# Second MLP products: a written TensorE order, weights made inside the step before, and their sums on VectorE

## The chip, the cores and the metric

The kernel runs on one core of a Trainium2 chip. A core has TensorE (PE in the profile) for matrix products, VectorE (DVE), ScalarE (ACT) and GpSimd (POOL) for elementwise work, and SyncE (SP), whose queue issues most transfers. The metric is device time in microseconds (us), the median of several runs.

## What is computed

Two sequences of 512 tokens and width 1024 pass a trunk of two layers in fp32. Layer 0 mixes tokens by a Fourier transform, layer 1 by attention; each is followed by the same kind of MLP:

```python
def sq_relu_mlp(h, w_up, w_down):
    a = jnp.maximum(h @ w_up, 0)
    return (a * a) @ w_down

# in trunk(), for each layer i
        x = x + fourier_mix(rms_norm(x, fourier_norm[j]), fourier_w_out[j])    # layer 0
        x = x + gqa_attention(rms_norm(x, attn_norm[j]), ...)                  # layer 1
        x = x + sq_relu_mlp(rms_norm(x, mlp_norm[i]), mlp_w_up[i], mlp_w_down[i])
```

`w_up` is 1024 x 4096 and `w_down` 4096 x 1024. The change is in the product with `w_down`, the second product of each MLP.

## The kernel before

**Arithmetic.** Every fp32 operand is split into a high and a low half (`split`, L81 to L83): ScalarE casts the high half (L82), VectorE subtracts it from the operand (L83). One fp32 product is three matmuls (high x high, high x low, low x high). `halves` (L98) splits a raw weight tile into a buffer of its own and gives back two operands.

**Seven products for eight.** Both MLP products are done by blocks of 2 x 2 with seven products in place of eight, and so need sums of blocks. The first product (`first_product`, L811) works by pairs of `D_FF` columns; of a pair's four results `Pair.out` (L914) makes the differences t1 to t4 on GpSimd (L918 to L921) and `put` (L815) writes seven activation operands, b11, b21, b22, t1 to t4, to DRAM: b ones from ScalarE's queue, t ones from SP's (L818).

**The second product** (`second_product`, L1036) runs over groups of pairs (four wide; layer 1 has one two wide) and, within a group, over four blocks of output columns, m = 0 to 3. A step (m, group) is of one of two kinds:

- `row` (L1084): the raw weights are split, and two products, with b11 and b21, add up in one bank of PSUM. The bank is read after the first into e (`add_e`), and after the second into the residual (`add`, L1055).
- `sums` (L1094): weights are summed, two sums by VectorE (L1098, L1099) and two by GpSimd (L1100, L1101), split, and five products follow in three banks: t2, t1, t3, b22, t4; t1 and b22 share a bank, and so do t3 and t4, each read twice by VectorE.

`add` and `add_e` are called evacuations below. A product is 12 matmuls of 128x512 (6 in a two-wide group). A row step goes with the sums step beside it; the sums of the last two column blocks of layer 0 have none, and of the first group all four rows come first, two at a time (`two_rows`, L1180). When a group begins, `group` (L1125) fetches its activation operands from DRAM (L1045, SP's queue) and splits them, all at once: two tiles of 128x1024 for each operand. With the last step of a column block, L1208 and L1209 add e, and `ready` begins the next layer's norm on that block (L87, squares on GpSimd at L155); `late` loads and splits weights of attention.

**What sets the order.** Each engine runs its instructions in order. The order is a scheduler's, which plans from estimated times, save within `manual_schedule(engines=...)`, where the named engines follow the code. In `second_product` only `two_rows` is written out so. Raw weights have five buffers, split ones four, PSUM eight banks, activations and residuals share 38.

Of the kernel before, what the change touches and what calls it, by code (L numbers as in the profile page):

```python
# [40 lines left out]
def trunk_kernel(ctx, tc, x_in, xt_in, y_out, dcos, dsin, feat, rope, gfour, gcol, grow, gfin,  # L41
# [56 lines left out]
    def halves(raw, n=512):  # L98
        hi, lo = own()
        split(hi[:, : 2 * n], lo[:, : 2 * n], raw)  # L100
        return [(hi[:, i * n : (i + 1) * n], lo[:, i * n : (i + 1) * n]) for i in range(2)]
# [709 lines left out]
    def first_product(l, blocks, rows, ahead):  # L811
# [3 lines left out]
        def put(op, p, src):  # L815
            for g, (p0, n) in enumerate(ROW_GROUPS[l] if op in ROW else SUM_GROUPS[l]):
                if p0 <= p < p0 + n:
                    (nc.scalar if op in ("b11", "b21", "b22") else nc.sync).dma_start(spill[l][op][g][p - p0], src)  # L818
# [7 lines left out]
        class Pair:  # L826
# [87 lines left out]
            def out(self, b11, b12, b21, b22):  # L914
# [3 lines left out]
                nc.gpsimd.tensor_sub(t[:, 0], b12, b11)  # L918
                nc.gpsimd.tensor_sub(t[:, 1], b22, t[:, 0])
                nc.gpsimd.tensor_sub(b12, b22, b12)  # L920
                nc.gpsimd.tensor_sub(t4, b21, t[:, 1])  # L921
                for op, x in (("b11", b11), ("b21", b21), ("b22", b22), ("t1", t[:, 0]), ("t2", t[:, 1]),
                              ("t3", b12), ("t4", t4)):
                    put(op, p, x)
# [85 lines left out]
        for p, pair in enumerate(pairs[:-1]):  # L1010
# [12 lines left out]
            pair.out(*done)  # L1023
# [12 lines left out]
    def second_product(l, blocks, rows, late=lambda: None, ready=lambda m: None):  # L1036
# [47 lines left out]
        def row(m, g, n, b):  # L1084
            x0 = residual(0, m)
            a11, a12 = rows_early.pop(m, None) or halves(row_raw(m, g, n), n * P)
            o = ps()
            product(o, a11, b["b11"])
            add_e(m, o)
            product(o, a12, b["b21"], False)  # L1090
            add(x0[:, 0], o)

        def sums(m, g, n, b):
            x0, x1 = residual(0, m), residual(1, m)  # L1094
            x, y = sums_raw(m, g, n)
            a12, a21, a11, a22 = x[:, 0], x[:, 1], y[:, 0], y[:, 1]
            s = rawp.tile([P, 2, n * P], F32, tag="raw", name=nm("raw"))
            nc.vector.tensor_add(s[:, 1], a21, a22)  # L1098
            nc.vector.tensor_sub(s[:, 0], s[:, 1], a11)  # L1099
            nc.gpsimd.tensor_sub(a11, a11, a21)  # L1100
            nc.gpsimd.tensor_sub(a12, a12, s[:, 0])  # L1101
            s2, s1 = halves(s, n * P)
            s3, a22 = halves(y, n * P)
            hi, lo = own()
            s4 = hi[:, : n * P], lo[:, : n * P]
            split(*s4, a12)
            o6, o5, o7 = ps(), ps(), ps()
            product(o6, s2, b["t2"])
            add_e(m, o6)
# [596 lines left out]
```

## Time and profile before

| | us |
|---|---|
| median of 3 runs | 1772.12 (1770.47 to 1773.23) |
| profiled execution, its own time | 1768.37 |
| its span | 1766.2 |
| TensorE busy | 1695.8 |
| VectorE busy | 1239.8 |
| ScalarE busy | 871.5 |
| GpSimd busy | 485.5 |

The profile is of one execution. In its second part (40 equal slices, each digit the busy share in tenths) TensorE reads 9 nearly throughout. The matmuls at L808 are those of both MLPs; layer 0's second products fill 431 to 760 us, layer 1's 1429 to 1707. A row of the timeline joins work of one line that runs without a break; the bracket at its end says how long the engine stood idle before it and which instruction released it.

### The profile page before, as it was taken

Reading aid. Unit: us, or ns where it says so; the run is one execution under the profiler, and the core shown is the slowest. Engines: PE = TensorE matmul, PEld = TensorE weight load, DVE = VectorE, ACT = ScalarE, POOL = GpSimd, SP = SyncE. Lnnn points to the kernel's source line nnn. Section 1 sums busy time; section 2 is a strip of 40 time slices with the busy share of each in tenths; the row PEclk is TensorE's granted clock in tenths of the full one; section 3 lists DMA queues with packets and bytes.
Section 4 is the critical chain, followed back from the end, with each engine's and each line's share of the span. In section 5 each row is a group of like instructions: output and inputs, shape, how many; then the busy total and the mean of one; then the engine's idle time right before and its main releaser. Section 6 shows DMA issues by size and latency. Waiting matters only on the chain. (4 is left out here: it accounts for less than half of the span.)

```text
span 1766.2 us, 22070 instructions
## 1 busy us (share of the span) xinstructions
PE 1695.8 (96%) x7870; PEld 1395.5 (79%) x7870; DVE 1239.8 (70%) x1775; ACT 871.5 (49%) x1530; POOL 485.5 (27%) x384
## 2 busy tenths in 40 slices
PE   4999999999899999999999999999999999999997
PEld 4887788888787877778877888787888877878776
DVE  8768876545967768976578843697655478686765
ACT  6666444446333424546687724554544554243234
POOL 3330443231412111543334302114322242111104
PEclk9999999999999999999999999999999999999999
DMA  9823454448744534430100212224544596355232
GB/s 278 226 95 120 178 192 177 163 167 293 259 167 157 202 130 179 153 117 25 48 25 1 92 53 113 95 103 185 200 149 153 200 321 225 136 208 177 85 108 96
DMA packets 104150, 267.13 MB, mean 151 GB/s; under 512 B 10200, under 2 KB 10200, under 8 KB 104040
## 3 DMA queue, kind: packets, MB, share of 16 engines
q1 hardware_dynamic: 88200, 234.78, 37.1%
q10 hardware_dynamic: 14112, 25.70, 3.8%
q0 software_dynamic: 1728, 5.24, 1.7%
q8 instruction: 62, 1.02, 0.2%
q14 instruction: 48, 0.39, 0.1%
HBM read 190.70 MB, written 73.92 MB: 150 GB/s over the span
## 5 line engine op out<-in xcount | busy, mean ns | idle before, releaser
L808 PE MATMUL ps<-u,w 128*128 128x512 f32 x4872 | 1130.6, 392 | 25.7 <-DVE u L1055 11.7
L808 PEld LDWEIGHTS ps<-u,w 128*128 128x128 f32 x4872 | 912.8, 189 | 236.4 <-issue 12.0
L82 ACT CAST w<-raw 128x1024 fp32r<-128x1024 f32 (+2 forms) x242 | 228.5, 954 | 498.3 <-PE ps L808 324.8
L83 DVE TENSOR_TENSOR w<-raw,w 128x1024 fp32r<-128x1024 f32 (+2 forms) x238 | 272.4, 1148 | 65.8 <-ACT w L82 64.8
L83 DVE TENSOR_TENSOR u<-u,u 128x1024 fp32r<-128x1024 f32 x133 | 180.4, 1374 | 18.4 <-ACT u L82 17.8
L1055 DVE TENSOR_TENSOR u<-ps,u 128x512 f32<-128x512 f32 x160 | 109.8, 687 | 92.6 <-PE ps L808 92.2
L82 ACT CAST u<-u 128x1024 fp32r<-128x1024 f32 x133 | 135.0, 1042 | 66.8 <-DMA u<-spill_b 53.1
L77 PE MATMUL ps<-u,u 128*128 128x512 f32 (+2 forms) x424 | 162.8, 386 | 2.1 <-DVE u L600 1.2
L1100 POOL TENSOR_TENSOR raw<-raw,raw 128x512 f32<-128x512 f32 (+1 forms) x32 | 46.9, 1466 | 425.5 <-DVE raw L1099 394.0
L78 PE MATMUL ps<-u,u 128*128 128x512 f32 (+2 forms) x424 | 158.1, 373 | 5.7 <-DVE u L83 5.4
L918 POOL TENSOR_TENSOR u<-u 128x512 f32<-128x512 f32 x30 | 40.2, 1340 | 436.4 <-ACT u L824 436.4
L79 PE MATMUL ps<-u,u 128*128 128x512 f32 (+2 forms) x424 | 157.9, 372 | 1.9 <-POOL u L83 1.4
L155 POOL TENSOR_TENSOR t<-t,t 128x512 f32<-128x512 f32 (+1 forms) x56 | 79.6, 1425 | 184.7 <-ACT t L153 128.7
L78 PEld LDWEIGHTS ps<-u,u 128*128 128x128 f32 x424 | 82.9, 195 | 18.6 <-DVE u L83 8.6
L79 PEld LDWEIGHTS ps<-u,u 128*128 128x128 f32 x424 | 82.5, 195 | 15.8 <-POOL u L83 2.0
L77 PEld LDWEIGHTS ps<-u,u 128*128 128x128 f32 x424 | 82.6, 195 | 14.3 <-DVE u L600 1.8
L83 DVE TENSOR_TENSOR u<-ps,u 128x512 fp32r<-128x512 f32 (+4 forms) x126 | 76.5, 627 | 17.3 <-ACT u L82 16.1
L808 PE MATMUL ps<-u,u 128*128 128x512 f32 x360 | 86.8, 390 | 1.8 <-DVE t L896 1.8
L881 DVE TENSOR_TENSOR t<-ps,u 128x512 f32<-128x512 f32 x30 | 20.8, 692 | 91.4 <-PE ps L808 89.9
L808 PEld LDWEIGHTS ps<-u,u 128*128 128x128 f32 x360 | 67.4, 188 | 16.8 <-issue 2.9
L82 ACT CAST u<-ps 128x512 fp32r<-128x512 f32 (+4 forms) x126 | 66.4, 542 | 25.6 <-PE ps L79 14.6
L791 DVE TENSOR_TENSOR u<-ps,u 128x512 f32<-128x512 f32 (+1 forms) x48 | 30.9, 645 | 65.3 <-PE ps L79 65.3
(221 smaller groups left out, 2079.9 us busy)
## 6 DMA issues: line engine op xcount, KB each, us to landing
raw<-w_up SPq DMA_DIRECT2D x82, 512.0 KB, 3.8
u<-spill_t SPq DMA_DIRECT2D x60, 512.0 KB, 6.2
raw<-w_sum SPq DMA_DIRECT2D x56, 512.0 KB, 3.7
spill_t<-u SPq DMA_DIRECT2D x90, 256.0 KB, 2.0
u<-spill_b SPq DMA_DIRECT2D x45, 512.0 KB, 5.8
spill_b<-t ACTq DMA_DIRECT2D x60, 256.0 KB, 2.0
raw<-w_row SPq DMA_DIRECT2D x28, 512.0 KB, 3.3
park<-u SPq DMA_DIRECT2D x24, 512.0 KB, 3.3
```

The source lines that it names most:

```text
L77: nc.tensor.matmul(out, lh, rh, start=first, stop=False)
L78: nc.tensor.matmul(out, lh, rl, start=False, stop=False)
L79: nc.tensor.matmul(out, ll, rh, start=False, stop=last)
L82: nc.scalar.copy(dst_hi, src)
L83: eng.tensor_sub(dst_lo, src, f32(dst_hi))
L155: nc.gpsimd.tensor_add(acc[q][:, :n], acc[q][:, :n], s[:, :n])
L791: nc.vector.tensor_add(x[:, :n], o[:, :n], x[:, :n])
L808: nc.tensor.matmul(o, w[x][:, sl], h[k][y], start=first and k + i == 0, stop=k == n - 1 and i == 2, skip_group_check=not first)
L881: nc.vector.tensor_add(u2, ob, t[:, 0])
L918: nc.gpsimd.tensor_sub(t[:, 0], b12, b11)
L1055: nc.vector.tensor_add(x, o, x)
L1100: nc.gpsimd.tensor_sub(a11, a11, a21)
```

## The change

`second_product` is written anew around two classes, `Row` and `Sums`, and a loop with TensorE's order written out:

- A step's products stand as: the row's first, t1, t3, the row's second, t2, b22, t4. Between the two products of a bank stand two others, or three where the step has a row.
- The next step's weights are made inside a step: its loads are issued after t1, its row is split after the row's second, three of its four sums are made and the first split after t2, the fourth after b22; the split of the third pair stands at the beginning of its own step.
- All four sums are VectorE's. Split weights of two-wide steps live in an activation slot (`narrow`).
- Activation operands change one at a time: `change` fetches the next group's operand behind the last product that uses it, and `hook`, called between products, splits it three calls later.
- At layer 0's beginning TensorE's, ScalarE's and VectorE's orders are written: the firsts of four rows, then their four seconds, with the first sums step's weights between.
- The last pair's differences go to VectorE, in both layers; the spills of t1 to t4 of layer 0's last pair but one go on GpSimd's queue; eight low halves of w_qkv (128x1024) go from GpSimd to VectorE.

The core of the diff:

```diff
-            def out(self, b11, b12, b21, b22):
+            def out(self, b11, b12, b21, b22, eng=nc.gpsimd, queue=nc.sync):
...
-                nc.gpsimd.tensor_sub(t[:, 0], b12, b11)
...
+                eng.tensor_sub(t[:, 0], b12, b11)
...
-            pair.out(*done)
+            pair.out(*done, queue=nc.sync if last or p < np_ - 2 else nc.gpsimd)
...
-            pairs[-1].out(*done)
+            pairs[-1].out(*done, nc.vector)
...
-            nc.gpsimd.tensor_sub(a11, a11, a21)
-            nc.gpsimd.tensor_sub(a12, a12, s[:, 0])
...
+            def sum_123(self):
+                a21, a11, a22 = self.x[:, 1], self.y[:, 0], self.y[:, 1]
+                s = self.s = rawp.tile([P, 2, self.n * P], F32, tag="raw", name=nm("raw"))
+                nc.vector.tensor_add(s[:, 1], a21, a22)
+                nc.vector.tensor_sub(s[:, 0], s[:, 1], a11)
+                nc.vector.tensor_sub(a11, a11, a21)
...
+            def sum_4(self):
+                nc.vector.tensor_sub(self.x[:, 0], self.x[:, 0], self.s[:, 0])
...
+        def change(op, i, g):
+
+            if g + 1 < len((ROW_GROUPS, SUM_GROUPS)[i][l]):
+                later.append([0, op, g + 1, fetch(op, g + 1, (ROW_GROUPS, SUM_GROUPS)[i][l][g + 1][1])])
...
+            with tc.manual_schedule(engines={ET.PE, ET.Activation, ET.DVE}):
+                for r in rows:
+                    r.load()
+                    r.split()
+                sums.load()
+                rows[0].first()
+                rows[1].first()
+                put(*there_later[0])
+                sums.sum_123()
+                sums.sum_4()
+                rows[2].first()
+                rows[3].first()
+                for r, step in zip(rows, (sums.split_12, sums.split_4, sums.split_3, lambda: None)):
+                    r.second()
+                    step()
...
+        def hook():
+            for x in later:
+                x[0] += 1
+            if later and later[0][0] > 2:
+                _, op, g, h = later.pop(0)
+                b.pop(op, None)
+                put(op, h)
+                held[op] = g
+
+        for k, (rows, sums) in enumerate(items):
+            nrows, nsums = items[k + 1] if k + 1 < len(items) else ([], None)
...
+            with tc.manual_schedule(engines={ET.PE}):
+                for r in rows:
+                    r.first()
...
+                for r in nrows:
+                    r.load()
+                if k:
+                    sums.split_3()
+                hook()
+                for i, op in enumerate(("t1", "t3", "t2", "b22", "t4")):
+                    sums.go(i)
+                    if sums.m == 3:
+                        change(op, 1, sums.g)
+                    if i == 0 and nsums:
+                        nsums.load()
+                    if i == 1:
+                        for r in rows:
+                            r.second()
...
+                        hook()
+                        for r in nrows:
+                            r.split()
+                    hook()
...
+                    if i == 2 and nsums:
+                        nsums.sum_123()
+                        nsums.split_12()
+                    if i == 3 and nsums:
+                        nsums.sum_4()
+                        nsums.split_4()
...
-        ws = wkv if cg == 2 else [load_w(w_qkv[cg, u], nc.gpsimd, home=own if u < 2 else lent) for u in range(4)]
+        ws = wkv if cg == 2 else [load_w(w_qkv[cg, u], home=own if u < 2 else lent) for u in range(4)]
```

How the order of instructions stands at three places (line, operation, out<-in by the program's names with their numbers, shape). `ps` is a bank, `w` a split weight, `raw` a raw or summed one, `u` an activation slot.

*The beginning of layer 0's second products.* Before, on VectorE, from the low halves of the last two rows' weights on:

```order
L83 TENSOR_TENSOR w_627_3947<-raw_597_3808,w_627_3947 128x1024
L83 TENSOR_TENSOR w_628_3963<-raw_599_3812,w_628_3963 128x1024
L1098 TENSOR_TENSOR raw_629_4014<-raw_606_3824,raw_607_3826 128x512
L1099 TENSOR_TENSOR raw_629_4014<-raw_629_4014,raw_607_3826 128x512
L83 TENSOR_TENSOR u_583_3694<-u_583_3694,u_582_3693 128x1024
L83 TENSOR_TENSOR u_585_3697<-u_585_3697,u_584_3696 128x1024
L83 TENSOR_TENSOR u_602_3817<-u_602_3817,u_601_3816 128x1024
L83 TENSOR_TENSOR u_604_3820<-u_604_3820,u_603_3819 128x1024
L1055 TENSOR_TENSOR u_581_3691<-ps_623_3878,u_581_3691 128x512
L83 TENSOR_TENSOR u_609_3829<-u_609_3829,u_608_3828 128x1024
L83 TENSOR_TENSOR u_611_3832<-u_611_3832,u_610_3831 128x1024
L1055 TENSOR_TENSOR u_598_3810<-ps_624_3879,u_598_3810 128x512
```

and on GpSimd, the sums of the first summed step and the last pair's differences:

```order
L1100 TENSOR_TENSOR raw_607_3826<-raw_607_3826,raw_606_3824 128x512
L1101 TENSOR_TENSOR raw_606_3824<-raw_606_3824,raw_629_4014 128x512
L918 TENSOR_TENSOR u_617_3860<-u_566_3606 128x512
L919 TENSOR_TENSOR u_617_3860<-t_593_3736,u_617_3860 128x512
L920 TENSOR_TENSOR u_566_3606<-t_593_3736,u_566_3606 128x512
L921 TENSOR_TENSOR t_618_3861<-t_596_3804,u_617_3860 128x512
```

After, on VectorE, behind the same two low halves:

```order
L922 TENSOR_TENSOR u_617_3860<-u_566_3606 128x512
L923 TENSOR_TENSOR u_617_3860<-t_593_3736,u_617_3860 128x512
L924 TENSOR_TENSOR u_566_3606<-t_593_3736,u_566_3606 128x512
L925 TENSOR_TENSOR t_618_3861<-t_596_3804,u_617_3860 128x512
L83 TENSOR_TENSOR u_583_3694<-u_583_3694,u_582_3693 128x1024
L83 TENSOR_TENSOR u_585_3697<-u_585_3697,u_584_3696 128x1024
L1126 TENSOR_TENSOR raw_627_3918<-raw_606_3824,raw_607_3826 128x512
L83 TENSOR_TENSOR u_602_3817<-u_602_3817,u_601_3816 128x1024
L1127 TENSOR_TENSOR raw_627_3918<-raw_627_3918,raw_607_3826 128x512
L83 TENSOR_TENSOR u_604_3820<-u_604_3820,u_603_3819 128x1024
L1128 TENSOR_TENSOR raw_607_3826<-raw_607_3826,raw_606_3824 128x512
L1134 TENSOR_TENSOR raw_606_3824<-raw_606_3824,raw_627_3918 128x512
```

The four differences and all four sums now stand on VectorE, ahead of or among the splits of the activation operands; GpSimd has no work in this stretch.

*A step with a row in layer 0's second group.* On TensorE, the first row of each product or part of one (ten or so rows follow it with the same bank). Before:

```order
L808 MATMUL ps_669_4329<-u_646_4184,w_668_4326 128x512
L808 MATMUL ps_677_4376<-u_576_3681,w_674_4367 128x512
L808 MATMUL ps_669_4329<-u_650_4194,w_668_4326 128x512
L808 MATMUL ps_677_4376<-u_577_3682,w_674_4367 128x512
L808 MATMUL ps_678_4377<-u_582_3693,w_674_4367 128x512
L808 MATMUL ps_679_4378<-u_601_3816,w_675_4370 128x512
L808 MATMUL ps_678_4377<-u_608_3828,w_676_4373 128x512
L808 MATMUL ps_679_4378<-u_612_3834,w_675_4370 128x512
```

After, in the same column block:

```order
L812 MATMUL ps_675_4354<-u_639_4075,w_670_4297 128x512
L812 MATMUL ps_678_4373<-u_576_3681,w_673_4318 128x512
L812 MATMUL ps_685_4397<-u_582_3693,w_677_4370 128x512
L812 MATMUL ps_675_4354<-u_646_4118,w_670_4297 128x512
L812 MATMUL ps_691_4437<-u_601_3816,w_673_4318 128x512
L812 MATMUL ps_678_4373<-u_608_3828,w_674_4335 128x512
L812 MATMUL ps_685_4397<-u_612_3834,w_677_4370 128x512
```

Before, a row's two products (bank 4329) stand three rows of matmuls apart, and t1 and b22 (4377) one product apart. Now the row's two (4354) have two products between, and so have t1 and b22 (4373) and t3 and t4 (4397).

*The end of layer 0's second products.* On VectorE, from the evacuations of the last step but one on; w_924 to w_926 before, and w_926 after, are weights of the last step. Before:

```order
L1098 TENSOR_TENSOR raw_923_6010<-raw_921_6006,raw_922_6008 128x512
L1055 TENSOR_TENSOR u_657_4236<-ps_905_5899,u_657_4236 128x512
L1099 TENSOR_TENSOR raw_923_6010<-raw_923_6010,raw_922_6008 128x512
L1209 TENSOR_TENSOR u_657_4236<-u_657_4236,t_621_3876 128x1024
L1055 TENSOR_TENSOR u_600_3814<-ps_906_5900,u_600_3814 128x512
L83 TENSOR_TENSOR w_924_6015<-raw_923_6010,w_924_6015 128x1024
L1208 TENSOR_TENSOR u_600_3814<-u_600_3814,t_621_3876 128x512
L83 TENSOR_TENSOR w_925_6018<-raw_922_6008,w_925_6018 128x1024
L87 SCALAR_TENSOR_TENSOR u_909_5974<-u_600_3814,gc_108,u_909_5974 128x512
L83 TENSOR_TENSOR w_926_6021<-raw_921_6006,w_926_6021 128x512
L87 SCALAR_TENSOR_TENSOR u_911_5981<-u_657_4236,gc_108,u_911_5981 128x512
L1055 TENSOR_TENSOR t_622_3877<-ps_927_6024,t_622_3877 128x512
```

After:

```order
L1059 TENSOR_TENSOR u_600_3814<-ps_907_5957,u_600_3814 128x512
L87 SCALAR_TENSOR_TENSOR u_912_6025<-u_600_3814,gc_108,u_912_6025 128x512
L1223 TENSOR_TENSOR u_600_3814<-u_600_3814,t_621_3876 128x512
L83 TENSOR_TENSOR w_926_6065<-raw_906_5955,w_926_6065 128x1024
L87 SCALAR_TENSOR_TENSOR u_914_6031<-u_600_3814,gc_108,u_914_6031 128x512
L1059 TENSOR_TENSOR u_666_4264<-ps_927_6068,u_666_4264 128x512
L87 SCALAR_TENSOR_TENSOR u_916_6038<-u_653_4150,gc_108,u_916_6038 128x512
L87 SCALAR_TENSOR_TENSOR u_918_6044<-u_653_4150,gc_108,u_918_6044 128x512
L1059 TENSOR_TENSOR u_666_4264<-ps_928_6082,u_666_4264 128x512
L83 TENSOR_TENSOR u_922_6054<-raw_920_6051,u_921_6053 128x1024
L83 TENSOR_TENSOR u_925_6060<-raw_923_6057,u_924_6059 128x1024
L1059 TENSOR_TENSOR t_622_3877<-ps_929_6096,t_622_3877 128x512
```

The sums of the last step stand earlier and are no longer among these rows; of its weights only the third pair (L83 on w_926) is left, behind the evacuations of the step before and two rows of the finished block's norm and sum.

## Rows read from the trace of the kernel before

**Rows 1.** Page, part 1: busy time, share of span, instructions.

```profile
PE 1695.8 (96%) x7870; PEld 1395.5 (79%) x7870; DVE 1239.8 (70%) x1775; ACT 871.5 (49%) x1530; POOL 485.5 (27%) x384
```

**Rows 2.** 50-us stretches: PE, PEld, DVE, ACT, POOL busy (count), clock, DMA share, GB/s.

```profile
450.00:500.00 50.00, 44.39 (x186) 35.91 (x185) 39.12 (x42) 13.10 (x14) 14.62 (x9) 0.93 0.59 216
500.00:550.00 50.00, 49.09 (x216) 39.94 (x215) 40.11 (x45) 20.86 (x23) 6.90 (x5) 1.00 0.51 182
700.00:750.00 50.00, 47.23 (x197) 37.39 (x196) 46.12 (x48) 23.60 (x35) 24.10 (x14) 0.97 0.43 149
1400.00:1450.00 50.00, 48.95 (x215) 39.74 (x214) 35.81 (x40) 29.68 (x42) 14.99 (x10) 1.00 0.96 345
1500.00:1550.00 50.00, 50.00 (x220) 40.96 (x219) 33.56 (x41) 16.81 (x19) 5.08 (x4) 1.00 0.46 166
```

**Rows 3.** Timeline of TensorE, 425 to 762: start, duration, work, [idle before].

```profile
430.72 22.60 PE L808 MATMUL ps<-u,w 128*128 128x512 f32 x99
458.93 81.10 PE L808 MATMUL ps<-u,w 128*128 128x512 f32 x345 [5.61 <-DVE w L83]
744.41 10.71 PE L808 MATMUL ps<-u,w 128*128 128x512 f32 x42
757.33 3.01 PE L808 MATMUL ps<-u,w 128*128 128x512 f32 x12 [2.21 <-DVE u L1055]
```

**Rows 4.** TensorE by line, 430 to 760: busy, mean ns | idle before.

```profile
L808 PE MATMUL ps<-u,w 128*128 128x512 f32 x1344 | 313.2, 394 | 15.4 <-DVE u L1055 8.1 <-DVE w L83 5.6 <-ACT w L82 1.6
```

**Rows 5.** Waits of TensorE, 395 to 735: us in total, times, longest.

```profile
PE ps L808 <- DVE w L83: 5.6, 1, 5.6
PE ps L808 <- DVE u L1055: 5.3, 6, 1.1
```

**Rows 6.** Waits of TensorE, 735 to 762.

```profile
PE ps L808 <- DVE u L1055: 2.9, 2, 2.2
PE ps L808 <- ACT w L82: 1.6, 2, 1.0
```

**Rows 7.** Waits of TensorE, 1390 to 1705, around layer 1's second products.

```profile
PE ps L808 <- DVE u L1055: 3.5, 5, 0.9
PE ps L808 <- DVE t L1055: 1.4, 1, 1.4
```

**Rows 8.** Timeline of VectorE (DVE), 440 to 475.

```profile
441.41 7.92 DVE L83 TENSOR_TENSOR u<-u,u 128x1024 fp32r<-128x1024 f32 x4
457.66 1.21 DVE L83 TENSOR_TENSOR w<-raw,w 128x1024 fp32r<-128x1024 f32 x1
```

**Rows 9.** Timeline of GpSimd (POOL), 435 to 475.

```profile
445.98 2.27 POOL L918 TENSOR_TENSOR u<-u 128x512 f32<-128x512 f32 x1
```

**Rows 10.** Timeline of SP's queue, 425 to 475.

```profile
455.37 0.88 SPq L91 DMA_DIRECT2D raw<-w_sum  x2
```

**Rows 11.** Groups by line and shape on VectorE, 430 to 760.

```profile
L83 DVE TENSOR_TENSOR w<-raw,w 128x1024 fp32r<-128x1024 f32 x47 | 63.0, 1344 | 10.6 <-ACT w L82 10.4
L1055 DVE TENSOR_TENSOR u<-ps,u 128x512 f32<-128x512 f32 x79 | 54.2, 686 | 44.2 <-PE ps L808 44.1
L87 DVE SCALAR_TENSOR_TENSOR u<-u,gc,u 128x512 fp32r<-128x512 f32 x13 | 16.8, 1295 | 0.8 <-ACT u L86 0.8
L1098 DVE TENSOR_TENSOR raw<-raw,raw 128x512 f32<-128x512 f32 x16 | 11.0, 688 | 5.7 <-DMA raw<-w_sum 5.4
L1209 DVE TENSOR_TENSOR u<-u,t 128x1024 f32<-128x1024 f32 x3 | 3.7, 1221 | 0.0
```

**Rows 12.** Groups by line and shape on GpSimd, whole span.

```profile
L1101 POOL TENSOR_TENSOR raw<-raw,raw 128x512 f32<-128x512 f32 x28 | 51.1, 1825 | 0.0
L383 POOL DMA_DIRECT2D u<-u x4 | 3.5, 875 | 16.8 <-DVE u L83 6.6 <-DVE t L387 4.7 <-DVE u L600 3.4
```

**Rows 13.** Page, part 6: DMA issues, KB each, median us to landing.

```profile
raw<-w_sum SPq DMA_DIRECT2D x56, 512.0 KB, 3.7
u<-spill_t SPq DMA_DIRECT2D x60, 512.0 KB, 6.2
```

More of the change, by code (lines that the diff above doesn't have):

```diff
@@ L1082, in sums_raw @@
             return [load_raw(w[:, i : i + 2], (P, 2, n * P)) for i in (0, 2)]
[L1084 to L1099, printed above, removed]
-            nc.gpsimd.tensor_sub(a11, a11, a21)
-            nc.gpsimd.tensor_sub(a12, a12, s[:, 0])
[L1102 to L1109, printed above, removed]
-            product(o5, s1, b["t1"])
-            add(x1[:, 1], o5)
-            product(o7, s3, b["t3"])
-            add(x1[:, 1], o7)
-            product(o5, s4, b["b22"], False)
-            add(x1[:, 0], o5)
-            product(o7, a22, b["t4"], False)
-            add(x0[:, 1], o7)
@@ L1120, in second_product, with __init__, load, split @@
-        steps = [(4 * p0 + m * n if l or i else 16 * g - 8 + 4 * m if g else m - 4, i, m, g, n)
+        class Row:
+            def __init__(self, m, g, n):
+                self.m, self.g, self.n = m, g, n
+            def load(self):
+                residual(0, self.m)
+                self.raw = None if self.m in rows_early else row_raw(self.m, self.g, self.n)
+            def split(self):
+                self.w = rows_early.pop(self.m, None) or halves(self.raw, self.n * P, (own, narrow)[self.n == 2])
+            def first(self):
+                self.o = ps()
+                assert held["b11"] == self.g
+                product(self.o, self.w[0], b["b11"])
+                add_e(self.m, self.o)
+            def second(self):
+                assert held["b21"] == self.g
+                product(self.o, self.w[1], b["b21"], False)
+                add(xs[0, self.m][:, 0], self.o)
@@ L1178, in ahead, with finish @@
                 residual(q, 1)
[L1180 to L1205 removed]
+        def finish(m):
             left[m] -= 1
@@ L1210, in second_product @@
                 ready(m)
+        first_product(l, blocks, rows, ahead)
+        e += [tm() for _ in range(4)]
+        items, waiting = [], []
+        for _, i, m, g, n in sorted(steps):
+            if i:
+                items.append((waiting, Sums(m, g, n)))
+                waiting = []
+            else:
+                waiting.append(Row(m, g, n))
+        assert not waiting
+        later = [[2, op, 0, h] for op, h in there_later[1:]]
+        def change(op, i, g):
+            if g + 1 < len((ROW_GROUPS, SUM_GROUPS)[i][l]):
+                later.append([0, op, g + 1, fetch(op, g + 1, (ROW_GROUPS, SUM_GROUPS)[i][l][g + 1][1])])
```

114 lines of the change are left out of this document (75 added, 39 removed).

## The prediction

> **What bounds the kernel now.** I read the busy shares first. TensorE is busy for 96% of the span, VectorE for 70%, GpSimd for 27% [rows 1], and the two orders hold the same matmuls, so only TensorE's idle time can be won. Dense stretches give its pace: 220 matmuls in 50 us [rows 2], 227 ns for one, 2.73 us for a product of twelve. The second table shows where it falls short: 186 matmuls in 450 to 500, at a granted clock of 0.93, and 197 in 700 to 750, at 0.97; both lie in layer 0's second products. Such a clock is a mean, of 2.4 GHz over most of the stretch and 1.2 over the rest. That stage runs from the row at 430.72 to the end of the row at 757.33 [rows 3], 329.6 us, for 1344 matmuls [rows 4], which want 305.5 at that pace: 24 us lie there.
>
> The waits name them. From 395 to 735 TensorE waits once for a weight's low half on VectorE, 5.6 us, and six times for an evacuation, 5.3 us together [rows 5]. The first wait has a tail: the 345 matmuls behind it take 81.10 us [rows 3] where the pace gives 78.4, so 2.7 us go to the lower clock after the idle time. In the last two steps it waits 2.9 us for evacuations and 1.6 for casts [rows 6], and the 42 matmuls in the row at 744.41 take 10.71 in place of 9.5: 5.7 us in all. In layer 1's second products I use 4.9 us, all evacuations [rows 7].
>
> The 5.6 us come from VectorE: at 441.41 four splits of 128x1024 take 7.92 us, 1.98 each, while the same split at 457.66 takes 1.21 [rows 8]; GpSimd was doing sums and the last pair's output differences then, 2.27 us for one [rows 9]. SP's queue waits for those differences too, and gets to the next summed weights at 455.37 only [rows 10].
>
> **Part by part.** The prices on VectorE are 0.69 us for an evacuation or sum and 1.21 to 1.34 for a split [rows 8, 11]; I use 1.22 for the latter.
>
> *The load moved.* 64 sums, eight output differences and eight low halves of w_qkv go from GpSimd to VectorE, 56 of the sums at 0.69 and 8 of half the width, some 42 us. A step with a row lasts 7 x 2.73 = 19.1 us on TensorE. On VectorE it then has 7 evacuations (4.8), 4 sums (2.8), three full splits and a half one (4.4): 12.0 us. A group of four such steps also splits 14 activation tiles (17.1): 65 of 76 us, against 59.5 before. The trace has 40.11 of 50 busy in 500 to 550 [rows 2]. VectorE keeps up with a step by 3 us or more, so I cost the sums there at nothing. Cover ends where groups change or a step has no row.
>
> *Start of layer 0's second products.* The eight row products last 21.8 us. By the order now shown, VectorE has in that time four differences and four sums (5.5), four activation splits (4.9), four evacuations (2.8), the low halves of two rows (2.4) and of the summed weights (3.1): 18.7 us, with no GpSimd beside it. The 5.6 us and the 2.7 of slow clock go: 8.3 won. Next is the second summed step, without a row: 13.6 us of TensorE against 5 evacuations, 4 sums, splits of 3.1 and the eight activation splits left (9.8), 19.2 us. It can cost 0 to 5.5; walking down the order I find TensorE ahead at one or two products, and take 1.5. The spills go out on SP as soon as VectorE is done, so the weights that waited until 455.37 come earlier; pair 14's four go on GpSimd's queue, whose own issues take 0.88 each [rows 12], and delay nothing that is needed soon: 0.
>
> *Product order and group changes.* Two products, or three, now stand between a bank's two, 5.5 us or more against an evacuation of 0.69. The six waits (5.3) go. In their place: an operand's next tile is fetched behind its last product and cast three products, 8.2 us, later, against 6.2 from issue to landing [rows 13]. The five summed operands' ten splits spread over two steps: 2 x 12.0 + 12.2 = 36.2 of 38.2 us. That fits by 2; if an evacuation that waits for its product holds a low half behind it, the price is one product, 2.7, at each of three changes. I take 0.3 each, since most have their next use a step later: 4.3 won, between -2.8 and 5.3.
>
> *End of layer 0's second products.* Two steps without a row, 13.6 us each: VectorE has 9.4 of evacuations, sums and splits, the finishing sums (1.22 [rows 11] and 0.69), four scaled splits between 0.69 and 1.30 [rows 11], and two w_qkv halves (2.4): 16.5 to 18.9 us. That is late by 5.8 to 10.6 over the two, of which up to 4.7, the last finish, may lie behind the last product: a price of 1.1 to 10.6 against 5.7 now. The four sums added cost 2.8; the four GpSimd sums gone (mean 1.83 [rows 12]) stretched splits by at most 0.77 each 1.98, about 2.8. I take 0, between -4.9 and 4.6.
>
> *Layer 1.* Its first four steps are two wide, 6.8 us of TensorE against 6.7 to 8.1 on VectorE (half-width sums and splits), so up to 5.2 late; its changes are as above. Of 4.9 I take 4 (-0.3 to 4.9), as loads and splits there now start a step earlier.
>
> *w_qkv.* Eight splits of 1.22, 9.8 at worst; VectorE's 70% leaves them room beside the projections: 0.
>
> **Sum.** 8.3 - 1.5 + 4.3 + 0 + 4 = 15.1 us. The profiled execution took 1768.4 us around a span of 1766.2, 3.7 under the median of 1772.1; there it would become 1753. Against the median: 1757.0.
>
> **Rivals.**
>
> *VectorE becomes the bound (slower).* It works in order, weights are made a single step ahead, and evacuations stand between them. If it overruns at the second step (5.5), at five group changes (2.7 each, 13.5), at the end (10.6), at layer 1's narrow steps (5.2), and the clock falls twice as it did (2.7 each), that is 40 us, against 24 of stalls removed. It decides once the eight places lose 3 us each. At three quarters, 30 us, the time is 1778. For it: 46.12 of 50 us busy in 700 to 750 [rows 2]. Against it: part of that is contention which goes. The Trainium skill, "Perfetto Trace Analysis", section Optimizing Scalar/DVE Operations, advises giving work from a saturated VectorE to ScalarE or even GpSimd, which is the opposite of this change and would mean this rival; it doubts itself there, since those two engines share a read port. I give it 0.13.
>
> *The wait only moves on.* TensorE no longer waits at the first summed product but pays 5.5 at the second step, loses 3 more at the end and wins 2 in layer 1: 8.3 - 5.5 + 4.3 - 3 + 2 = 6, giving 1766. For it: nothing in VectorE's total falls but contention. I give it 0.17.
>
> *Everything goes.* With GpSimd quiet, splits fall from 1.34 to 1.22 and no place is late: 8.3 + 5.3 + 4.6 + 4.9 = 23, or 1749. For it: the splits of 1.98. The Trainium skill, "SBUF — State Buffer", section Who interferes with whom, says that a VectorE instruction with two inputs in SBUF and a GpSimd one that reads SBUF exclude each other for a whole instruction; by that each GpSimd sum could cost VectorE its whole duration, more than its own sum costs, and this rival would be the forecast. The rows show less, 0.77 a split. I give it 0.12.
>
> *Transfers are late.* Operands are now fetched one at a time, behind their last use, into a queue whose engines are 0.96 busy in 1400 to 1450 [rows 2]. If each of five changes is late by a product (13.5), the gain is about 1.6: 1770.5. Against it: 8.2 us of lead over 6.2. I give it 0.08.
>
> That the change doesn't do what it says is ruled out by the order: the products, the sums and the differences stand where it puts them.
>
> **How the numbers follow.** Forecast 0.50 (1752 to 1763), the rivals 0.13, 0.17, 0.12, 0.08. A measurement here tells 0.2%, 3.5 us, from no change. Faster: 0.50 + 0.12 + two thirds of 0.17 = 0.73; same: the rest of 0.17 and 0.08, 0.14; slower: 0.13. The range reaches from 1747, just past the case in which everything goes, to 1771, which takes in the moved wait and the late transfers and leaves out the slower rival.
>
> **What would show it.** Right: no wait of TensorE over 2 us between 450 and 735, a clock of 1.00 there, VectorE's 128x1024 splits at 1.22, about 219 matmuls in each 50 us. Wrong: waits for low halves (VectorE) at the second summed step, at group changes or from 720 to 760 that together exceed 24 us; or TensorE waiting for casts whose tile had just landed (the transfers). If the stage still takes 329 us with VectorE above 90%, the load moved is the cause; if it falls by less than 6 us, the wait has moved on.

## The result and the profile after

| | before | after |
|---|---|---|
| median, first series | 1771.3 us (4 runs, 1770.3 to 1773.2) | 1740.1 us (4 runs, 1736.4 to 1740.6) |
| median, second series | 1770.5 us (9 runs) | 1738.4 us (4 runs, 1737.3 to 1739.3) |
| ratio after / before | | 0.9818 (95% interval 0.9801 to 0.9835); second series 0.9820 (0.9806 to 0.9834) |
| span of the profiled execution | 1766.2 us | 1738.6 us |

The kernel became 1.8% faster, some 31 us by medians and 27.6 by the two profiled spans. The forecast was 15 us and the range ended at 1747; the direction was right and the size half of what came.

The busy shares of after, which answer to [rows 1], and three stretches of 50 us that answer to [rows 2] (the columns are the same):

```profile
PE 1685.3 (97%) x7870; PEld 1396.4 (80%) x7870; DVE 1250.9 (72%) x1855; ACT 871.2 (50%) x1530; POOL 349.8 (20%) x308
```

```profile
450.00:500.00 50.00, 49.00 (x215) 39.83 (x214) 39.45 (x50) 14.74 (x16) 0.00 (x0) 1.00 0.45 167
500.00:550.00 50.00, 50.00 (x223) 41.39 (x222) 43.79 (x53) 22.74 (x24) 0.00 (x0) 1.00 0.57 201
700.00:750.00 50.00, 46.17 (x195) 37.38 (x195) 47.56 (x51) 25.65 (x36) 16.98 (x10) 0.97 0.51 185
```

VectorE's busy time rose by 11 us (1239.8 to 1250.9) though it took on 80 instructions, which take some 60 us there: 44.5 for the 64 sums (the forecast's 42), 5.6 for the eight differences, 10 for eight low halves at 1.22. What it had before thus became about 49 us shorter. GpSimd's busy time fell by 136. TensorE starts 215 matmuls in 450 to 500 at a clock of 1.00, where it was 186 at 0.93, and 500 to 550 is full.

TensorE's timeline in layer 0's second products, against [rows 3], and its waits from 395 to 762, against [rows 5, 6]:

```profile
430.27 39.03 PE L812 MATMUL ps<-u,w 128*128 128x512 f32 x170
470.30 253.26 PE L812 MATMUL ps<-u,w 128*128 128x512 f32 x1116 [1.00 <-DVE w L83]
725.08 3.02 PE L812 MATMUL ps<-u,w 128*128 128x512 f32 x12 [1.52 <-DVE w L83]
730.41 11.91 PE L812 MATMUL ps<-u,w 128*128 128x512 f32 x44 [2.31 <-DVE w L83]
```

```profile
PE ps L812 <- DVE w L83: 4.8, 3, 2.3
```

The wait of 5.6 us and its slow tail are gone, and so are all six evacuation waits: from 470.30 on TensorE runs 1116 matmuls without a break, 253.26 us or 227 ns each. Three waits for a low half are left, at the second summed step (1.00) and at the end (1.52 and 2.31, with a clock of 0.97 in 700 to 750 as before; in a second profile the same waits stand at a clock of 1.00). Layer 1's, against [rows 7]:

```profile
PE ps L812 <- DVE u L1059: 0.8, 1, 0.8
```

For what follows I use one measure that is steadier than the time: from the start of a stage's first L808 matmul (L812 after) to that of its last, less 0.227 us for each matmul of other work between. Back to back, at 0.2267 us from one matmul to the next, layer 0's stage would take 304.5 us and layer 1's 266.4; that is the pace. The kernel before took 328.6 and 276.0, 604.6 together (604.5 in a second profile), after took 312.1 and 268.3, 580.4 (578.6 in a second). So 24 of the 27.6 us lie in the two stages, 16.5 and 7.7. The other 3.4: the work between the stages is 0.8 shorter counted this way, the work behind the last 2.1 (two waits for weights at 1708, 0.9 and 0.5, no longer occur), and 0.5 lies ahead of the first.

### The profile page after: what moved, and what is told of

It reads as the page before. It is cut to its first block, busy times and chain, and to the rows that moved or that the text cites. A ratio compares the mean times of both kernels' runs of the same rounds, so it can differ in the third digit from the quotient of the medians.

```text
span 1738.6 us, 21980 instructions
## 1 busy us (share of the span) xinstructions
PE 1685.3 (97%) x7870; PEld 1396.4 (80%) x7870; DVE 1250.9 (72%) x1855; ACT 871.2 (50%) x1530; POOL 349.8 (20%) x308
## 5 line engine op out<-in xcount | busy, mean ns | idle before, releaser
L812 PE MATMUL ps<-u,w 128*128 128x512 f32 x4704 | 1083.9, 391 | 9.5 <-DVE w L83 5.0
L812 PEld LDWEIGHTS ps<-u,w 128*128 128x128 f32 x4704 | 882.5, 188 | 202.7 <-DVE t L889 7.8
L82 ACT CAST w<-raw 128x1024 fp32r<-128x1024 f32 (+1 forms) x226 | 219.6, 982 | 428.2 <-PE ps L812 268.4
L83 DVE TENSOR_TENSOR w<-raw,w 128x1024 fp32r<-128x1024 f32 (+1 forms) x226 | 260.1, 1153 | 54.7 <-ACT w L82 54.3
L83 DVE TENSOR_TENSOR u<-u,u 128x1024 fp32r<-128x1024 f32 x133 | 163.0, 1254 | 23.9 <-ACT u L82 23.9
L812 PE MATMUL ps<-u,u 128*128 128x512 f32 x528 | 126.9, 390 | 2.6 <-DVE t L900 1.8
L922 POOL TENSOR_TENSOR u<-u 128x512 f32<-128x512 f32 x28 | 36.1, 1289 | 414.9 <-ACT u L828 414.9
L812 PEld LDWEIGHTS ps<-u,u 128*128 128x128 f32 x528 | 98.6, 188 | 25.5 <-issue 2.9
L78 PEld LDWEIGHTS ps<-u,u 128*128 128x128 f32 x424 | 82.9, 195 | 18.0 <-DVE u L83 7.8
L79 PEld LDWEIGHTS ps<-u,u 128*128 128x128 f32 x424 | 82.5, 195 | 15.9 <-POOL u L83 2.1
L77 PEld LDWEIGHTS ps<-u,u 128*128 128x128 f32 x424 | 83.0, 196 | 13.8 <-ACT u L82 1.8
L83 DVE TENSOR_TENSOR u<-ps,u 128x512 fp32r<-128x512 f32 (+4 forms) x126 | 76.5, 627 | 17.8 <-ACT u L82 16.5
L827 ACT ACTIVATE t<-t 128x512 f32<-128x512 f32 x60 | 37.8, 631 | 56.1 <-DVE t L900 45.4
```

The lines of the kernel that those rows point to most:

```text
L77: nc.tensor.matmul(out, lh, rh, start=first, stop=False)
L78: nc.tensor.matmul(out, lh, rl, start=False, stop=False)
L79: nc.tensor.matmul(out, ll, rh, start=False, stop=last)
L82: nc.scalar.copy(dst_hi, src)
L83: eng.tensor_sub(dst_lo, src, f32(dst_hi))
L812: nc.tensor.matmul(o, w[x][:, sl], h[k][y], start=first and k + i == 0, stop=k == n - 1 and i == 2, skip_group_check=not first)
```

## The experiments

| kernel | median us | layer 0 | layer 1 | together |
|---|---|---|---|---|
| before | 1768.8 to 1771.4 in five series | 328.6 | 276.0 | 604.6 |
| before_quiet | 1748.2 | 312.2 | 271.6 | 583.8 |
| quiet_contend | 1769.5 | 327.2 | 277.2 | 604.4 |
| before_vsums | 1758.4 | 320.7 | 274.2 | 594.9 |
| after | 1740.1, 1738.4 | 312.1 | 268.3 | 580.4 |
| sums_back | 1743.8 | 312.6 | 270.5 | 583.2 |
| contend | 1744.4 | 314.3 | 269.2 | 583.5 |
| one_between | 1740.0 | 310.6 | 268.8 | 579.4 |
| sums_back_one | 1747.4 | 314.1 | 274.6 | 588.7 |
| group_at_once | 1741.1 | 312.1 | 268.6 | 580.7 |
| outs_back | 1743.2 | 312.1 | 270.1 | 582.2 |
| start_scheduled | 1738.1 | 308.8 | 267.8 | 576.6 |
| own_step | 1755.7 | 322.1 | 273.0 | 595.0 |
| joint_undo | 1750.1 | 317.2 | 272.1 | 589.2 |
| third_early | 1735.7 | 307.9 | 267.2 | 575.1 |
| best | 1736.8 | 306.2 | 267.3 | 573.5 |

Two profiles of the same kernel differ by up to 1.8 us in the last column, medians by 2 to 3.

The distance of a stage to its pace, by part. Layer 0's stage has three: the start (216 matmuls: eight row products and two steps without a row), the middle (1008: the twelve steps with a row) and the end (120: two steps without one).

| kernel | start | middle | end | layer 1 |
|---|---|---|---|---|
| before (second profile) | 8.0 (7.9) | 8.8 (7.4) | 7.3 (8.9) | 9.6 (9.4) |
| before_quiet | 0.3 | 3.9 | 3.5 | 5.2 |
| quiet_contend | 8.1 | 7.3 | 7.3 | 10.8 |
| before_vsums | 2.2 | 4.4 | 9.6 | 7.8 |
| after (second profile) | 1.6 (1.6) | -0.1 (-0.1) | 6.1 (4.4) | 1.9 (1.8) |
| sums_back | 1.6 | -0.1 | 6.6 | 4.1 |
| sums_back_one | 1.4 | -0.1 | 8.3 | 8.2 |
| own_step | 2.8 | -0.1 | 14.8 | 6.6 |
| joint_undo | 1.9 | 0.1 | 10.6 | 5.7 |

### Is the kernel before steady?

The kernel before and the changed kernel were run again, unedited.

> The kernel before once more, for a second profile: its first profiled execution took 1768.4 us where the timed runs took 1770.3 to 1773.2. Theory A (the stages are steady, the difference lies in the start or in the transfers): layer 0's second products again 329 to 330 us, layer 1's 278, and any difference from the first profile before 113 us. Theory B (the waits of TensorE scatter): the two stages differ from the first profile by 2 us or more.

> The changed kernel once more, beside the kernel before, since the kernel before came out at 1769 us in two later series after 1771 to 1772 in the first. Theory A (the first series drew the kernel before 2 us high): 1738 to 1741 against 1768 to 1770, a gain of 29 us, with layer 0's second products again 312 us and layer 1's 268.5. Theory B (the gain is 31 us or more): 1738 or less.

The stages came out at 328.6 and 275.8, within 0.2 us of the first profile: theory A. Its medians over five series are 1768.8 to 1771.4, so the 1772.1 of three runs against which the forecast was set was high by 1 to 3 us. The changed kernel repeated at 1738.4; beside 1770.5 that is 32 us, so of the two theories on after_again the second holds by the times, and the stages the first: 24 to 26 us there.

### What GpSimd's sums cost in the old order

Three edits of the kernel before, at L1100 and L1101.

```diff
 before_quiet: neither engine makes these two sums
-            nc.gpsimd.tensor_sub(a11, a11, a21)
-            nc.gpsimd.tensor_sub(a12, a12, s[:, 0])
 quiet_contend: GpSimd works as long, and nothing waits for it
+            nc.gpsimd.tensor_sub(a21, a21, s[:, 0])
+            nc.gpsimd.tensor_sub(a21, a21, s[:, 1])
 before_vsums: VectorE makes them
+            nc.vector.tensor_sub(a11, a11, a21)
+            nc.vector.tensor_sub(a12, a12, s[:, 0])
```

> The kernel before with nothing changed but all four weight sums on VectorE. Theory A (without the written order the sums only load VectorE where it is late already): between 3 us faster and 4 slower than the kernel before, 1768 to 1775. Theory B (contention was the larger part of the old stalls): 8 us faster or more, 1763 or less.

> The kernel before with the third and fourth weight sum of each step left out altogether (part of the computation is missing), so that neither GpSimd nor VectorE does them. Theory A (what the sums cost was GpSimd's hold on VectorE; the 42 us that VectorE takes on instead cost next to nothing): within 3 us of the run with the sums on VectorE, 1755 to 1760. Theory B (the added load does cost, and hides part of what the quiet gives): 5 us or more below that run, 1753 or less.

> The kernel before with its two GpSimd sums replaced by two GpSimd subtractions of the same size at the same places, whose results nothing uses (the third and fourth sums are missing from the computation): GpSimd holds VectorE up as before, but no weight waits for GpSimd. Leaving the sums out gave 1748. Theory A (the price of the old sums is GpSimd's hold on VectorE): 1764 or more, most of the 22 us back. Theory B (it is the weights' wait behind GpSimd): 1756 or less.

Without the sums (part of the result is missing then) the kernel before takes 1748.2 us, 22 less: theory B of before_quiet. With GpSimd working for nobody all of that comes back: 1769.5, ratio to before 0.9995 (0.9986 to 1.0004), theory A of quiet_contend. So the old sums cost 21 to 22 us, and none of it because weights waited for GpSimd. The table shows where: 7.7 at the start, 4.9 in the middle, 3.8 at the end, 4.4 in layer 1. Groups on VectorE from 430 to 760 (count | busy us, mean ns | idle before), of before_quiet and then quiet_contend, against 1344 ns for the second form in [rows 11]:

```profile
L83 DVE TENSOR_TENSOR u<-u,u 128x1024 fp32r<-128x1024 f32 x51 | 61.2, 1218 | 3.7 <-ACT u L82 3.4
L83 DVE TENSOR_TENSOR w<-raw,w 128x1024 fp32r<-128x1024 f32 x47 | 57.2, 1221 | 9.9 <-ACT w L82 9.6
```

```profile
L83 DVE TENSOR_TENSOR u<-u,u 128x1024 fp32r<-128x1024 f32 x51 | 70.9, 1406 | 2.9 <-ACT u L82 2.8
L83 DVE TENSOR_TENSOR w<-raw,w 128x1024 fp32r<-128x1024 f32 x47 | 62.4, 1332 | 9.6 <-ACT w L82 9.2
```

The stretch from 450 to 500 of before_quiet and of quiet_contend (columns as in [rows 2]), and TensorE's waits from 395 to 765 of before_quiet and of quiet_contend:

```profile
450.00:500.00 50.00, 50.00 (x221) 40.81 (x220) 35.99 (x44) 14.52 (x16) 0.00 (x0) 1.00 0.54 195
```

```profile
450.00:500.00 50.00, 44.50 (x186) 36.06 (x184) 38.88 (x42) 12.82 (x14) 14.44 (x9) 0.93 0.61 216
```

```profile
PE ps L808 <- DVE u L1055: 3.7, 4, 1.3
```

```profile
PE ps L808 <- DVE u L1055: 7.8, 8, 2.2
PE ps L808 <- DVE w L83: 5.5, 1, 5.5
```

With the sums gone the stretch is full and the 5.6-us wait does not occur, although loads and evacuations are the old ones. At the start the sums did more than run beside VectorE: they stood ahead of the last pair's differences on GpSimd, so all six ran from 441.6 to 455 beside VectorE's activation splits. Without them the differences run at once and are done when the splits begin. VectorE's four splits of [rows 8] and GpSimd's first difference of [rows 9], in before_quiet:

```profile
441.48 4.63 DVE L83 TENSOR_TENSOR u<-u,u 128x1024 fp32r<-128x1024 f32 x4
434.74 1.38 POOL L918 TENSOR_TENSOR u<-u 128x512 f32<-128x512 f32 x1 [10.60 <-DMA u<-park]
```

VectorE has no idle time in either kernel from those splits to the low half that TensorE waits for, and that half is begun at 452.36 in place of 457.66: the late queue of [rows 10] does not enter this wait. Over the stage VectorE's splits were stretched by 15 us in all (51 x 0.19 and 47 x 0.11), and TensorE lost 15 there; that the two sums agree is not shown to be more than chance, since part of TensorE's loss is slow clock.

On VectorE instead the same sums cost 11 us (594.9 against 583.8), 6.1 of them at the end, 2.6 in layer 1, 1.9 at the start and 0.5 in the middle. So in the old order the move is worth 10: theory B of before_vsums.

### Parts of the change undone one by one

```diff
 sums_back
-                nc.vector.tensor_sub(a11, a11, a21)
+                nc.gpsimd.tensor_sub(a11, a11, a21)
...
-                nc.vector.tensor_sub(self.x[:, 0], self.x[:, 0], self.s[:, 0])
+                nc.gpsimd.tensor_sub(self.x[:, 0], self.x[:, 0], self.s[:, 0])
 contend: VectorE's sums stay, and with them GpSimd runs
+                nc.gpsimd.tensor_sub(self.x[:, 1], self.x[:, 1], s[:, 0])
...
+                nc.gpsimd.tensor_sub(self.x[:, 1], self.x[:, 1], self.s[:, 1])
 one_between (from the second step on)
-                for i, op in enumerate(("t1", "t3", "t2", "b22", "t4")):
+                for i, op in enumerate(("t2", "t1", "t3", "b22", "t4") if k else ("t1", "t3", "t2", "b22", "t4")):
 group_at_once: change() fetches nothing; at the head of a step
+            for r in rows:
+                if r.m == 0 and r.g:
+                    group(0, r.g, r.n)
...
+            if sums.m == 0 and sums.g:
+                group(1, sums.g, sums.n)
...
 outs_back
-            pairs[-1].out(*done, nc.vector)
+            pairs[-1].out(*done)
 start_scheduled
-            with tc.manual_schedule(engines={ET.PE, ET.Activation, ET.DVE}):
+            with tc.manual_schedule(engines={ET.PE}):
 own_step: at the head of a step, in place of inside the one before
+                    if k:
+                        r.split()
...
+                    sums.sum_123()
+                    sums.split_12()
+                    sums.sum_4()
+                    sums.split_4()
                     sums.split_3()
```

> The changed kernel with the third and fourth weight sum of every step on GpSimd again. Theory A (written order and steps ahead carry the gain; the engine of the sums is worth little): 2 to 6 us slower than the changed kernel, 1742 to 1746, from two places where a low half is late. Theory B (a quiet GpSimd carries the gain): 12 us slower or more, 1752 and up, with waits at most group changes.

> The changed kernel with all its sums on VectorE and, in each step, two further GpSimd subtractions of 128x512 on a weight block that is no longer used: GpSimd's load on VectorE without any product waiting for GpSimd. Theory A (VectorE has 2 us or more to spare in most steps): 0 to 4 us slower than the changed kernel, 1740 to 1744, with VectorE's 128x1024 splits at 1.35 us mean in the second products. Theory B (contention was the larger part of the old stalls): 8 us slower or more.

> The changed kernel with the summed products in the old order (t2, t1, t3, b22, t4) from the second step on: one product in place of two between t1 and b22 and between t3 and t4; all else as changed. Theory A (the old stalls at group changes came from the evacuation between a bank's two products): 4 to 8 us slower than the changed kernel, 1744 to 1748, as waits of about 1 us for evacuations. Theory B (they came from VectorE's load alone): within 1 us, 1739 to 1741.

> The changed kernel with the activation operands of a group fetched and split all together at the group's beginning again, in place of one at a time. Theory A (spreading the ten or fourteen splits matters): 4 to 10 us slower than the changed kernel, 1744 to 1750, with the waits at the five group changes. Theory B (VectorE's room in the steps takes them in any order): within 2 us, 1738 to 1742.

> The changed kernel with the last pair's output differences on GpSimd again, in both layers. Theory A (these differences, by contention and by holding SP's queue, made the long wait at layer 0's first summed step): 5 to 9 us slower than the changed kernel, 1745 to 1749, with a wait of 3 us or more before 475 and a clock under 1.00 behind it. Theory B (the written order of the start carries it): within 2 us, 1738 to 1742.

> The changed kernel with only TensorE's order written at layer 0's start, and ScalarE's and VectorE's left to the scheduler, which puts the sums and all activation splits where it likes. Theory A (the written order of VectorE there removes the long wait): 4 to 8 us slower than the changed kernel, 1744 to 1748, with a wait of 3 us or more between 450 and 475. Theory B (the quiet GpSimd does): within 2 us.

Each of these gives back little. In the new order GpSimd's sums cost 2.8 us (sums_back, theory A), and GpSimd working for nobody 3.1 (contend; its time of 1744.4 is just above theory A): the hold alone is enough for it, and half the sums more or less on VectorE cannot be told from nothing. The spread of a group's operands is worth nothing (theory B). The differences of the last pair are worth 1.8 us, all of it in layer 1, where TensorE then waits 2.7 us once for a low half; the time of 1743.2 lies between the two theories, and the wait at layer 0's first summed step does not come back with them. Nor does it with VectorE's order there left to the scheduler, which is 2.0 to 3.8 us better in the stages, within the noise in time, and loses the wait at 470 too: layer 0's long wait came from GpSimd, as before_quiet shows, and the written order of that start does not help.

The order of the summed products alone is worth nothing either (theory B of one_between), but that edit undoes less than its text says. A row's second product still stands behind t1, so in a step with a row t1 and b22 keep two products between them (three in the changed kernel, one in the kernel before), and only t3 and t4 come down to one. The six old waits all stood before b22, in the first two steps of a group: the 444 matmuls ahead of the one at 540.94 [rows 3] are eight row products, two steps of 60, two of 84, and 60 more, and b22 is next. No run puts that place back as it was. What sums_back shows is that the new order as a whole needs no quiet GpSimd there, since the middle runs without a break (timeline as in [rows 3]):

```profile
467.98 258.91 PE L812 MATMUL ps<-u,w 128*128 128x512 f32 x1140 [1.09 <-DVE w L83]
```

### Parts undone together, and the step ahead

sums_back_one joins sums_back and one_between; joint_undo joins own_step, group_at_once and one_between.

> The changed kernel with both the third and fourth sum on GpSimd and one product in place of two between t1 and b22 and t3 and t4. Alone the first cost about 3 us and the second nothing. Theory A (each covers for the other: a late evacuation needs a VectorE held up by GpSimd and a short gap between the products): 8 to 12 us slower than the changed kernel, 1748 to 1752, with waits of about 1 us for evacuations at group changes. Theory B (the parts add up): 2 to 4 us slower, 1742 to 1744.

> The changed kernel with the sums and splits of a step's weights written at the beginning of that step again, in place of inside the step before; TensorE's order, the loads and the rest as changed. Theory A (making the weights a step ahead is what carries VectorE's added load): 8 us slower or more than the changed kernel's 1739, 1747 and up. Theory B (the scheduler puts VectorE's work there anyway): within 2 us.

> The changed kernel with three parts undone together: weights written in their own step, a group's operands changed all at once, one product between a bank's two. What stays of the change is TensorE's written order with a row's second product two products behind its first, the sums and differences on VectorE. Theory A (the parts cover for each other, as two of them did): 8 to 16 us slower than the changed kernel, 1747 to 1755, toward the 1758 of the sums moved alone. Theory B (TensorE's written order of rows carries the gain over that run): within 3 us, 1737 to 1742.

Product order and quiet GpSimd cover for each other: nothing for the one, 2.8 for the other, 8.3 for both (between the two theories in time, nearer theory A), at the end of layer 0 and in layer 1; the middle stays at its pace. Layer 1's waits for evacuations from 1370 to 1705, of one_between and of sums_back_one:

```profile
PE ps L812 <- DVE u L1059: 1.4, 1, 1.4
```

```profile
PE ps L812 <- DVE u L1059: 3.8, 3, 2.8
```

Making the weights a step ahead (a row's too) is the one part that counts alone: 14.6 us in the stages, 16 in time (theory A). Without it the stages take 595.0, as long as in before_vsums (594.9), where nothing but the sums was moved. So it is mainly the step ahead that pays for the moved sums; joint_undo, with 589.2, shows that the rest of the order can pay for a part. TensorE's waits in own_step from 395 to 765, and a row of its timeline in the last step of layer 0:

```profile
PE ps L812 <- DVE w L83: 7.1, 4, 3.6
PE ps L812 <- ACT w L82: 5.0, 2, 3.1
```

```profile
742.54 12.06 PE L812 MATMUL ps<-u,w 128*128 128x512 f32 x46 [3.58 <-DVE w L83]
```

In the steps with a row the weights come in time even so (middle -0.1); the loss lies in layer 1 (4.7) and in the steps without a row, where VectorE, by the forecast's count, has more than the 13.6 us that TensorE needs. joint_undo (theory A) is better than own_step by 5.6 us: with the old product order t2 and t1 share the first pair of weights, and the third pair is wanted a product later. That reason is argued from the code, no run isolates it.

### A faster version

```diff
 third_early
-                if k:
+                if k and not hasattr(sums, "s3"):
                     sums.split_3()
...
                         nsums.split_4()
+                        if not nrows:
+                            nsums.split_3()
 best: the same, with start_scheduled
```

> The changed kernel with the split of the third pair of weights moved into the step before, where that step is followed by one without a row. Theory A (the three waits left, 4.8 us at 470, 725 and 730, are this split standing behind evacuations and the norm's work in its own step): they go, 3 to 5 us faster than the changed kernel, 1735 to 1737. Theory B (VectorE is full there, whatever stands first): the waits move to the next low half or evacuation and the time stays within 1 us, 1739 to 1741.

> The changed kernel with two edits that each came out faster: the third pair's split in the step before where no row follows, and layer 0's start with only TensorE's order written. Theory A (their waits lie at different places, 1.2 us at 470 and 4.1 at 725 and 730, with their slow clock): 1732 to 1735. Theory B (one of them was noise): 1736 to 1738.

third_early takes 1735.7 us, 3 to 4 less than the changed kernel, though the intervals of the two ratios to before overlap (0.9793 to 0.9823 against 0.9806 to 0.9834); in the stages it has 575.1, 3.5 to 5.3 less. The time is that of theory A, but of its three waits only the one of 2.31 us is gone. best loses the wait at 470 as well and is down to 573.5, 2.6 above the pace; its median, 1736.8, is not to be told from 1735.7 and is theory B's. Of its waits one is left:

```profile
725.64 13.45 PE L812 MATMUL ps<-u,w 128*128 128x512 f32 x58 [1.52 <-DVE w L83]
```

## Why the prediction was wrong

**Term by term**, measured from both pairs of profiles (distance to the pace before, less that after):

| term | forecast won, us | measured |
|---|---|---|
| start of layer 0's second products | 8.3 - 1.5 = 6.8 | 6.3 to 6.4 |
| product order and group changes (the middle) | 4.3 | 7.5 to 8.9 |
| end of layer 0's second products | 0 | 1.2 to 4.5 |
| layer 1 | 4 | 7.7 |
| sum of these | 15.1 | 24.2 to 25.9 |
| outside the two stages | 0 | 3.4 (first pair) |

**The step that failed: the size of what was to be won.** That only TensorE's idle time in the second products could be won held for nearly all of the gain. But the terms 4.3 and 4 were read off waits that have a name. The text found 24 us in layer 0's stage and gave names to 19.3; the 4.8 left over entered no term and no bound, without a reason. In layer 1 it used 4.9 us of waits where the stage stood 9.6 above its pace. The two terms measured 7.5 to 8.9 and 7.7. What was left out were delays below 0.2 us: the wait at 540.94 has 0.91 us of idle and costs 1.07, and some matmuls start 0.04 to 0.11 us late where no wait is shown. Counted from the starts of layer 0's matmuls, those at the lower clock left aside, they come to 5.0 us before and 1.2 now. A range whose top is a sum of named waits could not reach 31. (5.3 less 0.3 at each of three changes is 4.4, not 4.3; nothing hangs on that slip.)

**GpSimd's hold: seen, and priced too low.** The text allowed it 8.3 us at the start and 2.8 at the end. Measured in the old order it cost 21, of which 4.9 lay in the middle and 4.4 in layer 1, where the text gave it nothing. The mean stretch of a split (1.34 against 1.22) and the 0.77 us at one place were read rightly; the step from there to the time was not.

**"I cost the sums there at nothing": this held.** In the twelve steps with a row the changed kernel is at its pace. In the old order the sums cost VectorE 11 us, nearly all of it where the text said that cover ends (the steps without a row, layer 1's narrow ones) and 0.5 in the middle; own_step shows that making weights a step ahead pays for them.

**Product order and group changes: the waits went as forecast, the cause is not isolated.** The text gave all six to the two products between a bank's two. A quiet GpSimd alone, in the old order, leaves two of them (0.77 and 0.97 us); the new order alone, with the sums on GpSimd, leaves none. So each is nearly enough, and which part of the new order does it stays open: one_between and joint_undo leave two products between t1 and b22 in a step with a row. At the end and in layer 1 their order is worth 5.5 us if GpSimd works and nothing if it does not.

**Start of layer 0's second products: right.** The wait and its tail went, and 1.00 us came at the second summed step. The cause was GpSimd, as the text said, but the share of the differences was too large in it: they hurt because the sums pushed them into VectorE's splits, and outs_back does not bring the wait back. The order written out there was not needed.

**End of layer 0's second products: the gain of 0 was a balance.** 4.5 us of waits became 3.8. Hold and load, taken as 2.8 each, measured 3.8 and 6.1 in the old order.

**Its own signs.** A clock of 1.00 and 223 matmuls in 500 to 550 came, and VectorE's splits fell to 1.22 (activations) and 1.26 (weights). A wait over 2 us stayed, at 730.

**The rivals.** VectorE as the bound did not come, but own_step shows how near it was: with the weights in their own step TensorE waits 12.1 us in layer 0 and 16 of the 31 us are lost. The Trainium skill ("Perfetto Trace Analysis", Optimizing Scalar/DVE Operations) says that giving work of a saturated VectorE to GpSimd may make sense and might not help; here, with VectorE 70% busy over the span, sums on GpSimd cost 3 us in the new order and 10 in the old. Nearest was "everything goes", to which the rule in the Trainium skill's "SBUF — State Buffer" (Who interferes with whom) pointed; the trace agrees with it in direction (a quiet GpSimd gave all 21 us), and shows 15 us of stretch for 55 us of GpSimd sums in layer 0's stage, not their whole duration. I gave that rival 0.12, and its 23 us had the same missing delays.

**The base.** The sum was set against 1772.1, the median of three runs; over five series the kernel before is at 1768.8 to 1771.4. From 1769.5 the same sum gives 1754, so 2 to 3 of the 17 us between forecast and result lie in the base.

## What to carry to other kernels

Where two engines contend, price the contention by taking the second engine's work away (or by letting it work for nobody), not by the mean stretch of an instruction. In layer 0's stage 15 us of stretch came with 15 us of TensorE's time in the old order; in the new one the stretch in contend (1320 and 1333 ns a split against 1263 and 1221, 9 us in all) came with 2 to 4. Look also at what the second engine's queue pushes into a bad moment. Bound a gain by the whole distance of a stage to its pace, and let the waits explain it afterwards; the small delays belong to them. Parts of a change that cover for each other look worthless when undone singly, so undo two together before calling a part idle, and see in the order of instructions that an undone part stands as it did.

## What the runs showed of the hardware

A VectorE split of 128x1024, which reads two operands from SBUF, took 1.22 us with GpSimd's sums out (before_quiet) and 1.33 to 1.41 in the mean with GpSimd working for nobody (quiet_contend); an evacuation, which reads one operand from PSUM, took 0.69 us in both, and ScalarE's casts 1.05.

Kernels whose instructions before the first MLP are the same start its product at 111.4 (third_early), 113.0 (the changed kernel) and 115.1 us (best). The rows are 60 to 115 us of the first and the last (columns as in [rows 2]):

```profile
60.00:115.00 55.00, 50.82 (x397) 48.45 (x397) 42.12 (x87) 35.49 (x79) 20.85 (x18) 1.00 0.60 170
```

```profile
60.00:115.00 55.00, 49.80 (x382) 48.03 (x381) 39.01 (x81) 34.12 (x75) 17.95 (x16) 0.94 0.55 150
```

The granted clock is a mean of 1.00 and 0.94 there, and 0.97 in the changed kernel: the first stays at 2.4 GHz, the others spend part of the stretch at 1.2. The starts spread by some 4 us, more than several parts of this change are worth; no run separates the clock's share from the rest. The comparison of stage lengths is free of this spread, though not of a fall of the clock inside a stage.
